# A state-space stage in a two-block kernel: where a branch GEMM and the next group's convolutions stand beside the preludes

## The chip, the cores and the metric

The program runs on one core of one Trainium2 chip as a single launch. The metric is the device time of an execution in microseconds (us). The core's engines each work through a queue of their own in order: TensorE (PE: matmuls and transposes), VectorE (DVE), ScalarE (ACT), GpSimd (POOL) and SyncE (SP, which issues the weight and row transfers). They meet through semaphores. Matmul results lie in PSUM banks, all other tiles in SBUF.

## The reference

512 tokens of width 1024 go through two blocks of two layers each, in float32. The first block (a hybrid mixer with a gated FFN) is not touched. A layer of the second block projects its input, and runs a state-space branch, a differential attention and a memory cross attention, which are gated, summed, projected and normalised. The stage in question is the state-space branch:

```
z, xbc, dt_raw, ... = split(x @ w_in)
xbc = silu(centred_depthwise_conv(xbc, conv_w, conv_b))      # 5 taps
xs, bm, cm = split(xbc)                                      # 32 heads of 64; 4 groups of 128 states
dt = softplus(dt_raw + dt_bias);  a = -exp(a_log)
y  = ssd_scan(xs*dt[fwd], dt[fwd]*a[0], bm, cm)              # chunks of 128 tokens
   + flip(ssd_scan(flip(xs*dt[bwd]), ...))                   # the same, backwards
   + d_skip * xs
y_ssd  = rmsnorm(y * silu(z)) * norm_w
merged = gate0 * (y_ssd @ w_br_ssd) + gate1 * ... + gate2 * ...
```

`ssd_scan` builds, for each chunk, a 128x128 decayed product of `cm` and `bm` that is applied to `xs`, and a state that is carried from chunk to chunk.

## The kernel before

**Layout.** Tiles are feature-major: 128 features on the partitions, the 512 tokens on the free axis. A full-precision GEMM is made of three passes over split operands (high by high L407, high of the weight by low of the input L408, low of the weight by high of the input L409), so a 1024-deep GEMM of one output tile is 24 matmuls of 128x512, and a 512-deep one is 12. Each weight block is loaded by SP into one of three `wraw` buffers, its high part is cast by ACT (L400) and its low part subtracted by DVE (L401).

**The stage.** `ssd` runs the 2048 inner channels in four groups g of 512 (four tiles `f` of 128 each, two heads to a tile). These are its pieces:

- `conv_x(g)`, 4 steps: a GEMM into a `pb` bank (two banks), the middle tap by ACT (L1347) and four taps by DVE (L1352) read from that bank into `svy`, silu by ACT (L1353) into `sxf`. `sxf` has seven buffers.
- `conv_bc(g)`, 2 steps: the same for `sbm` and `scm`, with GEMMs into a `pg` bank (two banks).
- `prelude(g)`, 11 steps. Steps 1 to 4, one for each chunk: four transposes of the `sxf` tiles into a `pb` bank (L429) and a copy by ACT to `sxt` (L1458). Step 5: transposes of `sbm` with a copy to `sbt` (L1465), and `cm`·`bm` products (L1469) which DVE masks (L1471, L1472). Steps 6 to 11, the state chain: DVE scales a chunk of `sxt` (L1481, into `st`, the `st2` buffers, four of them), PE multiplies by `sbt` (L1483, into `pm`), and DVE makes the new state: by a copy for the first one of each direction (L1486), else by adding (L1490) the older state that POOL has decayed (L1489). Directions alternate, three steps each.
- `ftiles(g)`, 16 steps, four for each of four tiles: the z GEMM with a silu (L1507), row loads, per head the decay exponents on ACT (L1517, L1518), min on DVE (L1521), exp on ACT (L1522), the masked product on POOL and DVE (L1519, L1520, L1523); then PE applies it (L1529, 8 matmuls) and the states (L1537, 6 matmuls), DVE, POOL and ACT finish the tile (L1531 to L1554) as a split pair `syp`.
- `branch(g)`, 4 steps of two 512-deep GEMMs each, from the group's four `syp` pairs into `pg` banks, copied by ACT (g = 0, L1565) or added by DVE (L1567) to the eight `merged` tiles `mg`.
- `gate_thread`, 8 gate GEMMs with sigmoid.

**What sets the order.** These pieces are generators. `weave` (L354 to L368) always advances the live one with the smallest `done/total`, and of equals the one that was named first. The order in which instructions are recorded so is their priority for a list scheduler at compile time, which works with costs of its own and may take a later one first where its operands are ready; on the chip each engine then runs its list in order. L1572 to L1592 say what is woven with what: decays with the first group's convolutions; then for each group `prelude(g)` with `branch(g-1)`, `ftiles(g)` with `conv_x(g+1)` (the gates for the last), and `conv_bc(g+1)` alone; then `branch(3)`.

Of the kernel before, what the change touches and what calls it, by code (L numbers as in the profile page):

```python
# [20 lines left out]
KD = 8  # L21
# [1303 lines left out]
def block2(c: Core, io, C, h, out, kvs, stop=None):  # L1325
# [18 lines left out]
    def conv(ps, cw, cb, m, res):  # L1344

        y = c.w(name="svy")
        A.activation(y, ps, AF.Identity, scale=cw[:, 2, m : m + 1], bias=cb[:, m : m + 1])  # L1347
        for tap in (0, 1, 3, 4):
            o = tap - 2
            d = slice(max(0, -o), S - max(0, o))  # L1350
            s = slice(max(0, o), S - max(0, -o))
            V.scalar_tensor_tensor(y[:, d], ps[:, s], cw[:, tap, m : m + 1], y[:, d], op0=ALU.mult, op1=ALU.add)  # L1352
        A.activation(res, y, AF.Silu)  # L1353
# [72 lines left out]
    def ssd(l, h, merged):  # L1426
# [10 lines left out]
        def conv_x(g):  # L1437
            for i in range(4):
                o = c.w(name="sxf")
                conv(proj(l, ("xbc", l, 4 * g + i), h, "pb"), cw, cb, 4 * g + i, o)  # L1440
                grp[g]["xf"].append(o)
                yield

        def conv_bc(g):
            for k, (nm, m) in enumerate((("sbm", 16 + g), ("scm", 20 + g))):
                o = grp[g][nm] = c.w(name=nm)
                conv(proj(l, ("xbc", l, m), h), cw, cb, m, o)
                yield
# [108 lines left out]
        def branch(g):  # L1557
            for j in range(4):
                hi, lo = c.load(("ws", l, g, j), 4)
                for i in range(2):  # L1560
                    m = 2 * j + i
                    ps = c.pg()
                    c.gemm_fm((hi[:, :, i * P : (i + 1) * P], lo[:, :, i * P : (i + 1) * P]), grp[g]["ys"], ps)
                    if g == 0:
                        A.copy(merged[m], ps)  # L1565
                    else:
                        V.tensor_tensor(merged[m], merged[m], ps, op=ALU.add)  # L1567
                yield

        gates = []  # L1570
        th = lambda gen, n: c.thread(gen, n, "S", "pm")
        with c.phase("ssd") as pool:  # L1572
            c.spare, c.spare_turn = pool, cycle(range(3))
            c.weave(th(decays(l, h, cdr, tm, d_fe, d_eo), 6), th(chain(conv_x(0), conv_bc(0)), 6))
            for g in range(4):
                c.weave(th(prelude(g), 11), th(branch(g - 1) if g else iter(()), 4))
                c.weave(th(ftiles(g), 16), th(conv_x(g + 1), 4) if g < 3 else th(gate_thread(l, 0, h, ["sxf"] * KD, gates), 7))
                if g < 3:
                    c.weave(th(conv_bc(g + 1), 2))
            c.weave(th(branch(3), 4))  # L1580
            ps = c.col_sums(sqa)
            v = c.small(NT)
            V.tensor_scalar(v, ps, 1.0 / 2048, 1e-5, op0=ALU.mult, op1=ALU.add)
            rs = c.rsqrt(v, NT)
            rbp = c.pm()
            c.row_bcast(rs, rbp)
            rb = c.w(name="sy1")
            V.tensor_copy(rb, rbp)
            for m in range(KD):
                V.tensor_tensor(merged[m], merged[m], gates[m], op=ALU.mult)  # L1590
                G.tensor_tensor(merged[m], merged[m], rb, op=ALU.mult)
            c.spare = None  # L1592

    def gate_thread(l, br, h, tags, out):
        for m in range(KD):
            out.append(gate(l, br, m, h, tags[m]))
            yield
# [343 lines left out]
    for l in range(DEPTH):  # L1941
# [22 lines left out]
        th = lambda gen: c.thread(gen, 8, "N", "pm")  # L1964
# [5 lines left out]
        else:  # L1970
# [8 lines left out]
            h = hn  # L1979
# [172 lines left out]
```

## Time and profile before

| | |
|---|---|
| three timed runs | 3864.66 to 3871.67 us, median 3867.84 us |
| profiled execution, own time | 3856.39 us |
| its span, first to last instruction | 3854.6 us |
| granted TensorE clock, mean (of 2.4 GHz) | 0.972 |
| PE busy | 3624.0 us, 94% |
| DVE, ACT, POOL busy | 63%, 47%, 20% |
| state-space stage, layer 0 | 1588 to 2046 us |
| state-space stage, layer 1 | 2735 to 3206 us |

A row of the timeline gives the start, the length, engine, line, operation, and in square brackets how long the engine stood idle before it and on what it waited. A row of the view of waits sums such idle time by the waiting line and the one that was waited for. Bank and buffer numbers are left out of the names. In the profile's program, a matmul of f32 operands other than the GEMMs' shows as two records.

### The profile page before, as it was taken

Reading aid. Unit: us, or ns where it says so; the run is one execution under the profiler, and the core shown is the slowest. Engines: PE = TensorE matmul, PEld = TensorE weight load, DVE = VectorE, ACT = ScalarE, POOL = GpSimd, SP = SyncE. Lnnn points to the kernel's source line nnn. Section 1 sums busy time; section 2 is a strip of 40 time slices with the busy share of each in tenths; the row PEclk is TensorE's granted clock in tenths of the full one; section 3 lists DMA queues with packets and bytes.
Section 4 is the critical chain, followed back from the end, with each engine's and each line's share of the span. In section 5 each row is a group of like instructions: output and inputs, shape, how many; then the busy total and the mean of one; then the engine's idle time right before and its main releaser. Section 6 shows DMA issues by size and latency. Waiting matters only on the chain. (4 is left out here: it accounts for less than half of the span.)

```text
span 3854.6 us, 51308 instructions
## 1 busy us (share of the span) xinstructions
PE 3624.0 (94%) x19000; PEld 2984.2 (77%) x19000; DVE 2431.1 (63%) x4355; ACT 1795.0 (47%) x3155; POOL 765.1 (20%) x877
## 2 busy tenths in 40 slices
PE   6888999998899999999999999999999999999998
PEld 4776887787777888777787887877777788887787
DVE  7986645567665333687866674337787766674336
ACT  5432422245323222677654664333776654664332
POOL 2331000003210000143432111003234332111003
PEclk9989999999899999999999999999999999999998
DMA  5711446642113233444433332323443433332222
GB/s 195 187 60 47 145 153 199 201 146 64 50 43 105 97 99 96 124 140 132 130 113 103 92 107 82 103 79 111 143 140 123 131 111 108 94 105 88 93 82 72
DMA packets 167419, 432.91 MB, mean 112 GB/s; under 512 B 30080, under 2 KB 49920, under 8 KB 167168
## 3 DMA queue, kind: packets, MB, share of 16 engines
q1 hardware_dynamic: 167168, 429.62, 36.0%
q8 instruction: 150, 2.46, 0.3%
q14 instruction: 101, 0.83, 0.1%
HBM read 396.24 MB, written 12.32 MB: 106 GB/s over the span
## 5 line engine op out<-in xcount | busy, mean ns | idle before, releaser
L400 ACT CAST whi<-wraw 128x1024 fp32r<-128x1024 f32 (+1 forms) x488 | 506.5, 1039 | 1037.0 <-PE pg L408 842.6
L401 DVE TENSOR_TENSOR wlo<-wraw,whi 128x1024 fp32r<-128x1024 f32 (+1 forms) x488 | 640.9, 1314 | 403.4 <-ACT whi L400 388.6
L407 PE MATMUL pg<-h,whi 128*128 128x512 f32 (+1 forms) x2192 | 876.6, 400 | 15.6 <-ACT h L400 10.7
L409 PE MATMUL pg<-h,wlo 128*128 128x512 f32 (+1 forms) x2192 | 862.0, 393 | 6.6 <-DVE wlo L401 6.6
L408 PE MATMUL pg<-h,whi 128*128 128x512 f32 (+1 forms) x2192 | 862.6, 394 | 4.3 <-POOL h L401 4.3
L407 PEld LDWEIGHTS pg<-h,whi 128*128 128x128 f32 (+1 forms) x2192 | 412.5, 188 | 107.5 <-ACT h L400 13.4
L409 PEld LDWEIGHTS pg<-h,wlo 128*128 128x128 f32 (+1 forms) x2192 | 412.6, 188 | 99.2 <-DVE wlo L401 13.6
L408 PEld LDWEIGHTS pg<-h,whi 128*128 128x128 f32 (+1 forms) x2192 | 412.9, 188 | 94.8 <-POOL h L401 7.4
L407 PE MATMUL pg<-whi,h 128*128 128x256 f32 (+1 forms) x640 | 187.8, 295 | 15.8 <-ACT whi L400 10.9
L408 PE MATMUL pg<-wlo,h 128*128 128x256 f32 (+1 forms) x640 | 186.4, 292 | 11.6 <-DVE wlo L401 11.4
L401 POOL TENSOR_TENSOR gp<-mraw,gp 128x256 fp32r<-128x256 f32 x32 | 25.4, 813 | 864.1 <-ACT gp L400 864.1
L409 PE MATMUL pg<-whi,h 128*128 128x256 f32 (+1 forms) x640 | 184.0, 288 | 0.0
L409 PE MATMUL pg<-gp,wlo 128*128 128x512 f32 (+1 forms) x432 | 159.9, 370 | 0.9 <-DVE wlo L401 0.9
L407 PE MATMUL pg<-gp,whi 128*128 128x512 f32 (+1 forms) x432 | 159.7, 370 | 0.0
L408 PE MATMUL pg<-gp,whi 128*128 128x512 f32 (+1 forms) x432 | 159.6, 369 | 0.0
L407 PE MATMUL pg<-yp,whi 128*128 128x512 f32 (+2 forms) x368 | 142.7, 389 | 6.2 <-ACT whi L400 2.9
L408 PE MATMUL pg<-yp,whi 128*128 128x512 f32 (+2 forms) x368 | 142.8, 389 | 3.6 <-DVE yp L401 3.6
L409 PE MATMUL pg<-yp,wlo 128*128 128x512 f32 (+2 forms) x368 | 142.2, 388 | 2.9 <-DVE wlo L401 2.9
L407 PEld LDWEIGHTS pg<-whi,h 128*128 128x128 f32 x640 | 124.3, 195 | 23.1 <-ACT whi L400 13.1
L1519 POOL TENSOR_SCALAR st<-scl,stm 128x128 f32<-128x128 f32 x256 | 124.2, 504 | 89.5 <-PE pm L1529 89.5
L408 PEld LDWEIGHTS pg<-wlo,h 128*128 128x128 f32 x640 | 124.7, 195 | 16.3 <-DVE wlo L401 14.3
L530 DVE CUSTOM_DVE_ANT_0 wraw<-wraw,cond 128x1024 f32<-128x1024 f32 x80 | 100.7, 1263 | 54.9 <-DMA wraw<-in_wflat_dram 54.8
(585 smaller groups left out, 7601.7 us busy)
## 6 DMA issues: line engine op xcount, KB each, us to landing
wraw<-in_wflat_dram SPq DMA_DIRECT2D x595, 512.0 KB
srf<-dram SPq DMA_DIRECT2D x64, 256.0 KB
sre<-dram SPq DMA_DIRECT2D x64, 256.0 KB
seo<-dram SPq DMA_DIRECT2D x128, 96.0 KB
araw<-in_wflat_dram SPq DMA_DIRECT2D x16, 512.0 KB
rsw<-rr SPq DMA_DIRECT2D x128, 64.0 KB
wraw<-in_wflat_dram SPq DMA_DIRECT2D x16, 384.0 KB
mraw<-in_mem_dram SPq DMA_DIRECT2D x40, 128.0 KB
```

The source lines that it names most:

```text
L400: self.nc.scalar.copy(hi, src)
L401: (eng or self.nc.vector).tensor_tensor(lo, src, hi.bitcast(F32), op=ALU.subtract)
L407: mm(out, ah, bh, start=start, stop=False)
L408: mm(out, ah, bl, start=False, stop=False)
L409: mm(out, al, bh, start=False, stop=stop)
L530: V.tensor_tensor_reduce(r, r, cond, 1.0, 0.0, ALU.mult, ALU.add, mod[:, j : j + 1])
L1519: G.tensor_scalar(t2[:, sl], cbl[:, ch], dtt[:, ch, hh : hh + 1], 1.0, op0=ALU.mult, op1=ALU.mult)
```

## The change

The four pieces that are woven with the tiles are made ahead of the loop (`nxt`). In the first group, `conv_x(1)` is now woven with `prelude(0)`, counted as three steps (`total = 3`), until the prelude ends; what is left of it is woven with the first group's tiles. In the other groups the branch of the group before starts with `done = -1`, so that one of its steps is taken ahead of the prelude's first.

```
         c.weave(th(decays(l, h, cdr, tm, d_fe, d_eo), 6), th(chain(conv_x(0), conv_bc(0)), 6))
+        nxt = [th(conv_x(1), 4), th(conv_x(2), 4), th(conv_x(3), 4), th(gate_thread(l, 0, h, ["sxf"] * KD, gates), 7)]
         for g in range(4):
-            c.weave(th(prelude(g), 11), th(branch(g - 1) if g else iter(()), 4))
-            c.weave(th(ftiles(g), 16), th(conv_x(g + 1), 4) if g < 3 else th(gate_thread(l, 0, h, ["sxf"] * KD, gates), 7))
+            pre = th(prelude(g), 11)
+            if g:
+
+                tb = th(branch(g - 1), 4)
+                tb.done = -1
+                c.weave(pre, tb)
+            else:
+                nxt[0].total = 3
+                c.weave(pre, nxt[0], until=pre)
+                nxt[0].total, nxt[0].done = 4 - nxt[0].done, 0
+            c.weave(th(ftiles(g), 16), nxt[g])
             if g < 3:
                 c.weave(th(conv_bc(g + 1), 2))
```

With prelude steps P1 to P11, branch steps B1 to B4 and convolution steps X1 to X4, the recorded order changes as follows. First group: before P1 to P11, later one X with each tile; now P1 X1 P2 to P4 X2 P5 to P8 X3 P9 to P11, and X4 with the first tile. Other groups: before P1 B1 P2 P3 B2 P4 to P6 B3 P7 to P9 B4 P10 P11; now B1 P1 B2 P2 P3 B3 P4 to P6 B4 P7 to P11.

What the scheduler made of it stands below at three places; "..." is for rows left out. On PE, the first group's prelude in layer 0 (`sxf`, `sbm`: operands of transposes; `h` with `pg_13889` or `pg_14006`: the first tile's z GEMM). Before, the transposes and the start of the z GEMM:

```order
L429 MATMUL pb_13795<-k_1_60,sxf_13509 128x128
...
L429 MATMUL pb_13795<-k_1_60,sxf_13666 128x128
L429 MATMUL pb_13802<-k_1_60,sxf_13509 128x128
...
L429 MATMUL pb_13809<-k_1_60,sxf_13509 128x128
...
L429 MATMUL pb_13809<-k_1_60,sxf_13666 128x128
L407 MATMUL pg_13889<-h_13320,whi_13892 128x512
L429 MATMUL pb_13816<-k_1_60,sxf_13509 128x128
...
L408 MATMUL pg_13889<-h_13320,whi_13892 128x512
...
L429 MATMUL pb_13824<-k_1_60,sbm_13711 128x128 x4
```

Now, with two GEMMs of the second group's convolutions (`pb_13803`, `pb_13863`) among the same transposes:

```order
L429 MATMUL pb_13795<-k_1_60,sxf_13509 128x128
...
L429 MATMUL pb_13795<-k_1_60,sxf_13666 128x128
L407 MATMUL pb_13803<-h_13320,whi_13806 128x512
...
L409 MATMUL pb_13803<-h_13341,wlo_13807 128x512
L429 MATMUL pb_13841<-k_1_60,sxf_13509 128x128
...
L429 MATMUL pb_13841<-k_1_60,sxf_13666 128x128
L407 MATMUL pg_14006<-h_13320,whi_14009 128x512
...
L408 MATMUL pg_14006<-h_13329,whi_14009 128x512
L429 MATMUL pb_13848<-k_1_60,sxf_13509 128x128
...
L409 MATMUL pg_14006<-h_13329,wlo_14010 128x512
...
L407 MATMUL pb_13863<-h_13320,xhi_13866 128x512
...
L429 MATMUL pb_13902<-k_1_60,sbm_13711 128x128 x4
```

The first and second convolution GEMM stand within the transposes, and the third and fourth follow among and behind the state matmuls, all ahead of the first tile's L1529; before, the first of them stood right ahead of that L1529, and each of the others with one of the next tiles. By the whole list, ACT's table loads in the program go from 211 to 221, six of the added ones in the last group of layer 0; every other engine has the same instructions as before.

On PE, the start of the fourth group in layer 0 (`sxf`: transposes; `syp`: the third group's branch GEMMs). Before:

```order
L409 MATMUL pg_16421<-h_13341,xlo_16425 128x512
L429 MATMUL pb_16459<-k_1_60,sxf_15812 128x128
...
L429 MATMUL pb_16500<-k_1_60,sxf_15812 128x128
...
L429 MATMUL pb_16507<-k_1_60,sxf_15812 128x128
...
L429 MATMUL pb_16548<-k_1_60,sxf_15812 128x128
...
L429 MATMUL pb_16548<-k_1_60,sxf_16286 128x128
L407 MATMUL pg_16472<-syp_15901,whi_16468 128x512
L408 MATMUL pg_16472<-syp_15901,whi_16468 128x512
```

Now:

```order
L409 MATMUL pg_16421<-h_13341,xlo_16425 128x512
L429 MATMUL pb_16493<-k_1_60,sxf_15812 128x128
...
L429 MATMUL pb_16493<-k_1_60,sxf_16286 128x128
L429 MATMUL pb_16534<-k_1_60,sxf_15812 128x128
L429 MATMUL pb_16534<-k_1_60,sxf_15970 128x128
L407 MATMUL pg_16465<-syp_15901,whi_16461 128x512
...
L409 MATMUL pg_16465<-syp_16375,wlo_16462 128x512
L429 MATMUL pb_16534<-k_1_60,sxf_16128 128x128
...
L429 MATMUL pb_16541<-k_1_60,sxf_15812 128x128
...
L429 MATMUL pb_16541<-k_1_60,sxf_16128 128x128
L407 MATMUL pg_16479<-syp_15901,whi_16461 128x512
```

The branch GEMMs, which followed all sixteen transposes, now stand after six of them and after eleven. Layer 1's fourth group has the same two orders, and its third group went from eleven ahead of the first GEMM to seven. Layer 0's third group had six ahead of its first GEMM, and four between that and the second, before; it has seven and three now.

On PE, the end of the state chain in the third group of layer 0 (`st` with `sbt`: the state matmuls; `syp`: branch; `h`: the first tile's z GEMM). Before:

```order
L409 MATMUL pg_15663<-syp_15441,wlo_15646 128x512
L1483 MATMUL pm_15679<-st_3347_15677,sbt_15621 128x512
L1483 MATMUL pm_15685<-st_3350_15683,sbt_15621 128x512
L1483 MATMUL pm_15693<-st_3354_15691,sbt_15621 128x512
L407 MATMUL pg_15705<-syp_14967,whi_15701 128x512
...
L409 MATMUL pg_15719<-syp_15441,wlo_15702 128x512
L1483 MATMUL pm_15735<-st_3363_15733,sbt_15621 128x512
L1483 MATMUL pm_15743<-st_3367_15741,sbt_15621 128x512
L407 MATMUL pg_15755<-h_13320,xhi_15758 128x512
```

Now:

```order
L409 MATMUL pg_15697<-syp_15441,wlo_15680 128x512
L1483 MATMUL pm_15713<-st_3352_15711,sbt_15655 128x512
L1483 MATMUL pm_15719<-st_3355_15717,sbt_15655 128x512
L1483 MATMUL pm_15727<-st_3359_15725,sbt_15655 128x512
L1483 MATMUL pm_15735<-st_3363_15733,sbt_15655 128x512
L407 MATMUL pg_15755<-h_13320,xhi_15758 128x512
...
L409 MATMUL pg_15755<-h_13326,xlo_15759 128x512
L1483 MATMUL pm_15743<-st_3367_15741,sbt_15655 128x512
L407 MATMUL pg_15755<-h_13329,xhi_15758 128x512
```

The 24 branch matmuls (22 of their rows are left out above) that stood between the third state matmul and the last two are gone from there, and nine of the z GEMM's stand ahead of the last one. On DVE, at the same place (`shs`: states; `st_3367`: the last state matmul's operand). Before:

```order
L401 TENSOR_TENSOR wlo_15817<-wraw_15814,whi_15816 128x1024
L1486 COPY shs_15681<-pm_15679 128x512
L1490 TENSOR_TENSOR shs_15687<-shd_15688,pm_15685 128x512
L1490 TENSOR_TENSOR shs_15695<-shd_15696,pm_15693 128x512
L1481 TENSOR_TENSOR st_3367_15741<-sxt_15571,stm_13471 128x512
L1520 SCALAR_TENSOR_TENSOR st_3380_15792<-scu_15634,stm_13470,st_3380_15792 128x128 x4
```

Now:

```order
L401 TENSOR_TENSOR wlo_15917<-wraw_15914,whi_15916 128x1024
L1486 COPY shs_15715<-pm_15713 128x512
L1490 TENSOR_TENSOR shs_15721<-shd_15722,pm_15719 128x512
L1490 TENSOR_TENSOR shs_15729<-shd_15730,pm_15727 128x512
L1490 TENSOR_TENSOR shs_15737<-shd_15738,pm_15735 128x512
L1481 TENSOR_TENSOR st_3367_15741<-sxt_15605,stm_13471 128x512
L1520 SCALAR_TENSOR_TENSOR st_3380_15792<-scu_15668,stm_13470,st_3380_15792 128x128 x4
```

One more state addition stands ahead of the last scaling (L1481). The second to fourth groups of both layers have this new pattern, six places in all.

## Rows read from the trace of the kernel before

**Rows 1.** The page's first part: busy time of PE and its weight loads.
```profile
PE 3624.0 (94%) x19000; PEld 2984.2 (77%) x19000; DVE 2431.1 (63%) x4355; ACT 1795.0 (47%) x3155; POOL 765.1 (20%) x877
```
**Rows 2.** Windows: length, then busy of PE, PEld, DVE, ACT, POOL; clock; DMA.
```profile
1621.00:1705.00 84.00, 78.46 (x405) 62.00 (x404) 74.27 (x116) 68.41 (x131) 39.19 (x51) 0.98 0.45 134
2766.00:2852.00 86.00, 78.29 (x401) 61.01 (x399) 77.05 (x117) 70.12 (x136) 38.81 (x51) 0.98 0.43 133
1656.00:1705.00 49.00, 44.55 (x239) 36.61 (x238) 43.69 (x64) 45.32 (x89) 19.25 (x20) 0.97 0.59 172
```
**Rows 3.** Waits of PE, first group of layer 0, 1621 to 1705 us.
```profile
PE pm L1529 <- DVE st L1523: 2.7, 1, 2.7
PE pg L407 <- DVE svy L1352: 1.6, 1, 1.6
```
**Rows 4.** Waits of PE, first group of layer 1, 2766 to 2852 us.
```profile
PE pm L1529 <- DVE st L1523: 2.7, 3, 2.1
PE pg L407 <- DVE svy L1352: 2.3, 2, 1.9
```
**Rows 5.** Waits of PE, later groups of layer 0: total, times, longest.
```profile
PE pg L407 <- DVE svy L1352: 5.7, 1, 5.7
PE pb L429 <- ACT sxt L1458: 3.5, 1, 3.5
PE pb L429 <- ACT sxf L1353: 3.3, 1, 3.3
```
**Rows 6.** Waits of PE, later groups of layer 1, 2853 to 3206 us.
```profile
PE pb L429 <- ACT sxt L1458: 8.8, 2, 5.3
PE pb L429 <- ACT sxf L1353: 6.4, 2, 4.8
```
**Rows 7.** Timeline of PE, starts of the third and fourth group, layer 0.
```profile
1805.30 0.77 PE L407 MATMUL pg<-syp,whi 128*128 128x512 f32 x1 [5.66 <-DVE svy L1352]
...
1906.77 1.33 PE L429 MATMUL pb<-k,sxf 128*128 128x128 f32 x5 [3.34 <-ACT sxf L1353]
1911.60 1.97 PE L429 MATMUL pb<-k,sxf 128*128 128x128 f32 x8 [3.50 <-ACT sxt L1458]
1913.72 0.80 PE L407 MATMUL pg<-syp,whi 128*128 128x512 f32 x1
```
**Rows 8.** Timeline of DVE, start of the fourth group, layer 0.
```profile
1908.55 1.53 DVE L1352 SCALAR_TENSOR_TENSOR svy<-pg,c,svy 128x510 f32<-128x510 f32 x2 [0.44 <-ACT svy L1347]
...
1912.92 1.40 DVE L1352 SCALAR_TENSOR_TENSOR svy<-pg,c,svy 128x510 f32<-128x510 f32 x2
```
**Rows 9.** Groups of instructions by line: DVE, state-space stage of layer 0.
```profile
L401 DVE TENSOR_TENSOR wlo<-wraw,whi 128x1024 fp32r<-128x1024 f32 x42 | 56.6, 1350 | 14.7 <-ACT whi L400 14.7
L1352 DVE SCALAR_TENSOR_TENSOR svy<-pb,c,svy 128x511 f32<-128x511 f32 (+1 forms) x63 | 46.7, 742 | 9.4 <-ACT svy L1347 9.2
```
**Rows 10.** Timeline of PE, state chain of the third group, layer 0.
```profile
1828.36 2.73 PE L1483 MATMUL pm<-st,sbt 128*128 128x512 f32 x6
1830.53 0.79 PE L407 MATMUL pg<-syp,whi 128*128 128x512 f32 x1
...
1836.40 1.88 PE L1483 MATMUL pm<-st,sbt 128*128 128x512 f32 x4
```
**Rows 11.** Timeline of DVE, the same state chain.
```profile
1832.41 0.69 DVE L1490 TENSOR_TENSOR shs<-shd,pm 128x512 f32<-128x512 f32 x1 [0.58 <-POOL shd L1489]
1833.02 0.93 DVE L1481 TENSOR_TENSOR st<-sxt,stm 128x512 f32<-128x512 f32 x1
```
**Rows 12.** Timeline of POOL, the same state chain.
```profile
1831.32 2.08 POOL L1489 TENSOR_TENSOR shd<-shs,scd 128x512 f32<-128x512 f32 x2 [5.11 <-DVE shs L1486]
```
**Rows 13.** Timeline of ACT, a table load and what follows it.
```profile
1894.87 1.28 ACT L1522 ACT_TABLE_LOAD   x1
1896.16 0.63 ACT L1522 ACTIVATE sre<-sre 128x512 f32<-128x512 f32 x1
```
**Rows 14.** Windows, as rows 2: last group's tiles of layer 0.
```profile
1945.00:1998.00 53.00, 53.00 (x285) 43.79 (x284) 40.51 (x61) 38.15 (x65) 20.38 (x31) 1.00 0.46 144
```

## Prediction

> **What bounds the kernel now.** I read the busy shares first: PE is busy 3624.0 us of a span of 3854.6 [rows 1], so it sets the time, and reordering pays only where PE stands idle. I then took the view of waits for PE, stretch by stretch through the state-space stage. Three kinds of wait are there to be won or lost.
>
> In the first group, PE waits for the products of a tile (L1529 for L1523) 2.7 us in each layer, and for a `pg` bank that the taps of `conv_bc` still read 1.6 and 2.3 us [rows 3, 4]. The windows of this group say what stands behind: 84 us with PE busy 78.46 and DVE 74.27, and 86 us with 78.29 and 77.05 [rows 2]. DVE is as good as full in layer 1, and in the tiles (1656 to 1705 us, 49 us) PE has 44.55, DVE 43.69 and ACT 45.32: all three are near their limit.
>
> At the starts of the later groups PE waits for the last convolution's silu (`sxf`), for the copy that frees a `pb` bank (`sxt`), or for the taps that free a `pg` bank: 5.7 + 3.5 + 3.3 = 12.5 us in layer 0 and 8.8 + 6.4 = 15.2 us in layer 1 [rows 5, 6]. These are the largest waits that the change touches.
>
> The third kind is absent: at the end of the state chain the last two state matmuls start right behind the 24 branch matmuls, without idle time [rows 10].
>
> **The change part by part.** No engine but ACT gets another instruction, so each term is a wait that goes, stays or comes.
>
> *First group.* Three of four convolution GEMMs leave the stretch behind L1529 of the first tile; the first stood ahead of it already. A GEMM of 24 matmuls takes 5.87 us, read from the 24 between 1830.53 and 1836.40 [rows 10], so 17.6 us of PE's work leave the tiles. With them go 4 x 0.742 + 1.35 = 4.3 us of DVE's work each [rows 9], 13.0 us in three. Does the prelude have holes for it? Hardly: the waits listed for this group lie in the tiles and at its end, and the z GEMM and the first convolution were in the prelude already. So work is exchanged: the prelude grows by what the tiles lose. In the tiles the `conv_bc` GEMMs, recorded behind them, are drawn forward as cover for PE, so that their taps are done earlier; the wait for their `pg` bank at the group's end should go. That is 1.6 in layer 0 and 1.9 (the longest of the two) in layer 1: **-3.5 us**. The waits of L1529 I leave as they are: the tile's row work still ends last. Bounds: all waits of rows 3 and 4 go, 4.3 + 5.0 = -9.3; or the tiles fall to the pace of DVE, 17.6 - 13.0 = 4.6 in each layer, +9.2. SP's loads for the three GEMMs go out earlier too, ahead of the tiles' row loads; three `wraw` buffers hold them, and I cost this at nothing as long as the tiles' rows, which are asked for as before, come in time. One buffer matters: `sxf` has seven, so the silu of the fourth convolution waits for the first tile's L1531, with ACT's queue behind it. That is part of the upper bound.
>
> *Starts of the later groups.* The branch GEMMs move to between the transposes. A branch GEMM needs a `pg` bank, and both banks hold `conv_bc` results that DVE is still tapping: at the fourth group of layer 0 DVE is at these taps from 1908.55, and a pair of them still runs at 1912.92 to 1914.32 [rows 8]. PE's first branch GEMM starts at 1913.72 [rows 7]. So when it is asked for after six transposes, at about 1908, it can hardly start sooner than it did behind sixteen; the wait of 3.50 for the copy becomes a wait for taps, and the ten transposes left come behind it. By that replay the start costs 1 or 2 us more. Another row says the contrary: the third group of layer 0 has had the new order all along, and pays 5.66 for the taps [rows 7] and next to nothing besides, against 3.34 + 3.50 = 6.84 at the fourth group. If the three starts in the old order (6.84 in layer 0, 15.2 for two in layer 1) came down to 5.7 to 6 each, that would be -4.0. I take half: **-2 us**. Bounds: all of 22.0 goes, for banks that are free in time; or +2 at each of three, +6.
>
> *State chain.* Here a cover is taken away. Call S the start of the first state matmul of the last batch, 1828.36. Before, three state matmuls end the batch at S + 2.17 and 24 branch matmuls follow until S + 8.04 [rows 10]. In that time DVE makes two additions and the last scaling, which ends at 1833.95, S + 5.6 [rows 11]: 2.4 us to spare. Now PE has four state matmuls, 4 x 0.72 = 2.9 us, and nine of the z GEMM's, 9/24 of 5.87 = 2.2 us, and wants the last one at S + 5.1. And DVE has one addition more ahead of the scaling; it needs the second decay by POOL, which ended at 1831.32 + 2.08 = 1833.40 [rows 12]. So the addition runs from 1833.40 to 1834.1 (0.69), the scaling to 1835.0 (0.93): S + 6.6. PE waits 6.6 - 5.1 = 1.5 us, and what is queued behind it is the rest of the z GEMM and, through it, the first tile. There are six such places: 9 us if all are alike. The trace shows one chain, with DVE held up by a weight split just ahead of it; where no split stands there, DVE is ahead and nothing is lost. Bounds 0 and +9; I take the middle, **+4.5 us**.
>
> *ACT's table loads.* Ten more are in the list, six of them in the last group of layer 0. In the trace the load takes 1.28 us and the exp behind it starts at 1896.16, one hundredth after its end [rows 13]. In that group's tiles ACT has 38.15 us of 53.00 [rows 14]; with 6 x 1.28 = 7.7 it has 45.9, still under PE's 53. Nothing. The Trainium skill (*ScalarE: Activation LUTs*, section *What ACT_TABLE_LOAD costs*) adds a drain to each switch and comes to about 2.66 us; by that estimate the six would bring ACT to 54.1 us, 1.1 us over PE's, and the sum would be 1.1 us longer. The trace has no such gap between load and exp, so the row is followed.
>
> *Sum.* -3.5 - 2 + 4.5 = -1.0 us. The durations are those of the profiled execution, whose own time of 3856.39 us (span 3854.6, 1.8 us around it) is 11.45 us under the median of the timed runs, 3867.84. A change in waits carries over as it is: 3867.84 - 1.0 = 3866.8, about **3867 us**.
>
> **The rivals.** *The starts are covered (faster).* If a branch GEMM between the transposes gives ACT time for the copies, the waits for `sxt` go, 3.5 + 8.8 = 12.3 us. For it: at 1911.60 PE waits 3.50 us for a copy while branch matmuls lie ready. Against it: the bank that DVE frees no sooner. With -3.5 in the first group and the chain at half its middle value, +2.3: -12.3 - 3.5 + 2.3 = -13.5, 3854 us.
>
> *The first group's tiles lose their cover (slower).* The mechanism is DVE's and ACT's pace in the tiles once the convolution GEMMs are gone from there: they keep 4.6 us more than PE in each layer, PE idles in front of L1529, and DVE at 77.05 of 86 us has no room to have worked ahead in the prelude. Price 9.2, with the chain at 4.5 and nothing won at the starts: +13.7, 3882 us. It decides where the waits in front of the first group's L1529 pass some 6 us a layer, against 2.7 now. For it: the tight windows. Against it: in the prelude the heads' rows can be made ahead, as far as their buffers go.
>
> *Nothing moves.* The scheduler had drawn the z GEMM and the first convolution into the prelude already, and the third group of layer 0 had nearly the new order; the rest may just exchange one wait for another of the same length. 3868 us.
>
> **How the numbers follow.** Below 0.2%, 7.7 us, this kernel's measurement tells no change. I give my forecast 0.38, with a range of its own of 3860 to 3875; the faster rival 0.31, the slower one 0.22, nothing moving 0.09. Faster by over 0.2%: nearly all of the faster rival (0.29) and 0.04 of the forecast, 0.33. Slower: 0.20 of the slower rival and 0.03 of the forecast, 0.23. The rest, 0.44, is no change that can be told. The outer bounds are -9.3 - 22 = -31.3 and 9.2 + 6 + 9 = +24.2; for 8 in 10 the range reaches to the rivals and a little past the faster one, 3850 to 3883 us.
>
> **What would show it.** In the changed kernel's waits of PE: for the first group, no wait for taps at its end, and L1529's near 2.7 us a layer (above 6, the slower rival). For the fourth group of layer 0, a branch GEMM that starts near 1913.7 less the shift up to there, with a wait for L1352 in front of it (if it starts two us or more sooner, the faster rival). At each of the six chains, a wait of L1483 for L1481 of about 0.8 us on the mean; none at all would strike that term, 1.5 at each would double it. A prediction off by more than a few us in either direction, with the waits of PE in this stage unchanged, would mean that something else than these three places decides, such as transfers that come later for SP's changed order.

## The result, and the profile after

The changed kernel takes 3908.55 us, median of four runs (3906.87 to 3913.39), against 3866.25 us, median of four, for the kernel before: a ratio of 1.0116, with a 95% interval of 1.0101 to 1.0130. That is 42 us slower, outside the predicted range of 3850 to 3883 us.

The page's first part, after, beside [rows 1]: of the span's 57 us more (3911.6, against 3854.6), PE is busy 30 us longer for the same 19000 records, and idle 27 us longer.

```profile
PE 3654.2 (93%) x19000; PEld 3005.2 (77%) x19000; DVE 2430.0 (62%) x4355; ACT 1809.8 (46%) x3165; POOL 763.2 (20%) x877
```

To see where, I cut the stage at places that have the same work ahead of them in both lists. The table is worked out from the timelines of PE; each pair is layer 0 / layer 1, in us. "First group" runs from its first transpose to the second group's first L1529; the next two from one group's first L1529 to the next one's; "last group" from its first L1529 to the first L451 behind the branch.

| kernel | first group | second | third | last group | sum |
|---|---|---|---|---|---|
| before | 123.8 / 127.1 | 104.1 / 104.8 | 105.9 / 107.5 | 87.9 / 87.9 | 421.7 / 427.3 |
| after | 132.2 / 147.4 | 104.6 / 104.5 | 105.4 / 107.3 | 94.2 / 92.9 | 436.3 / 452.1 |
| branch_first | 125.1 / 127.6 | 106.4 / 105.4 | 105.8 / 106.5 | 92.7 / 94.5 | 429.9 / 434.0 |
| branch_first_g12 | 125.1 / 127.6 | 105.8 / 105.4 | 105.3 / 105.2 | 88.0 / 87.9 | 424.1 / 426.1 |
| branch_first_gate_exp | 125.1 / 128.8 | 106.2 / 106.1 | 106.1 / 106.0 | 92.5 / 91.4 | 430.0 / 432.3 |
| branch_first_dve_mult | 123.4 / 125.9 | 103.8 / 103.7 | 104.1 / 103.9 | 90.7 / 90.9 | 421.9 / 424.3 |
| conv_early | 130.9 / 144.4 | 105.1 / 104.5 | 107.0 / 107.0 | 87.9 / 88.0 | 430.9 / 443.9 |
| one_conv_early | 132.3 / 134.5 | 104.4 / 103.9 | 106.6 / 106.9 | 87.9 / 88.0 | 431.3 / 433.2 |
| conv_early_dve_mult | 127.6 / 134.9 | 102.4 / 103.5 | 103.1 / 103.7 | 87.5 / 87.5 | 420.7 / 429.7 |
| conv_early_z_exp | 133.6 / 138.9 | 109.4 / 107.8 | 106.8 / 106.1 | 88.6 / 89.0 | 438.4 / 441.8 |
| after_dve_mult | 128.9 / 135.6 | 104.3 / 101.9 | 104.2 / 105.4 | 90.7 / 90.7 | 428.1 / 433.5 |
| after_dve_chain | 130.1 / 137.7 | 100.3 / 101.9 | 101.0 / 101.5 | 87.5 / 87.5 | 419.0 / 428.5 |
| before_dve_mult | 122.0 / 127.9 | 104.0 / 102.9 | 104.1 / 103.1 | 87.5 / 87.5 | 417.6 / 421.5 |
| before_dve_chain | 118.8 / 127.2 | 100.8 / 102.0 | 100.5 / 100.7 | 87.5 / 87.5 | 407.7 / 417.4 |
| branch_in_pm | 123.1 / 126.1 | 96.9 / 96.6 | 102.9 / 103.0 | 91.9 / 91.9 | 414.9 / 417.6 |

The stage is 14.6 + 24.8 = 39.4 us longer, nearly all of the 42 us by which the medians differ. The first group loses 8.4 and 20.2 us, the last group 6.3 and 5.0. (A group's row holds the start and the state chain of the group behind it.) The second and third groups, with the starts and state chains that two of the three terms of the prediction were about, are even within 0.6 us. (The two profiled executions differ by another 18 us ahead of and behind the stage, where the instructions are the same; the medians do not show that.)

**The first group.** The windows of its prelude and its tiles, layer 0 and then 1, and the last group's tiles of layer 0 (columns as in [rows 2]):

```profile
1627.00:1665.00 38.00, 36.45 (x161) 27.46 (x160) 29.37 (x44) 23.78 (x41) 12.17 (x20) 1.00 0.21 69
1665.00:1716.00 51.00, 41.64 (x237) 31.95 (x237) 42.89 (x68) 35.51 (x70) 24.65 (x31) 1.00 0.49 144
2786.00:2830.00 44.00, 37.38 (x160) 28.43 (x159) 31.78 (x45) 28.06 (x52) 12.16 (x20) 0.96 0.27 82
2830.00:2884.00 54.00, 46.51 (x235) 36.34 (x234) 42.47 (x69) 33.76 (x66) 23.58 (x30) 0.87 0.41 132
1969.00:2034.00 65.00, 60.88 (x324) 49.44 (x323) 36.20 (x48) 47.12 (x70) 23.30 (x28) 0.97 0.39 121
```

In layer 0 the prelude takes 38 us where it took 21, by its three GEMMs of about 5.5 us each, 16.6 us. The tiles (first L1529 to the end of their GEMMs) take 50 where they took 59.5, so only 9.5 of the 16.6 us come back. DVE is busy 42.9 of 51 us and ACT 35.5, so neither is full, and PE idles 9 us. PE's waits in these tiles of layer 0, to be read against [rows 3]:

```profile
PE pm L1529 <- DVE st L1523: 3.2, 3, 1.4
PE pg L409 <- DVE xlo L401: 3.1, 1, 3.1
PE pg L409 <- DVE wlo L401: 1.6, 1, 1.6
PE pg L407 <- ACT szs L1507: 1.5, 1, 1.5
```

And in the first group of layer 1, beside [rows 4]:

```profile
PE pb L429 <- ACT sxt L1458: 9.2, 2, 5.8
PE pm L1529 <- DVE st L1523: 5.2, 3, 2.9
```

The whole first group, before and after in layer 0 and then in layer 1 (columns as in [rows 2]), shows that the two layers lose in different ways:

```profile
1621.30:1745.00 123.70, 118.16 (x577) 92.68 (x575) 101.66 (x160) 93.20 (x172) 52.17 (x71) 0.99 0.42 126
1627.20:1759.30 132.10, 119.62 (x577) 90.86 (x575) 104.01 (x159) 91.12 (x169) 51.68 (x71) 1.00 0.38 114
2765.80:2892.90 127.10, 119.19 (x577) 92.39 (x575) 106.66 (x165) 95.49 (x182) 51.78 (x71) 0.99 0.42 127
2786.00:2933.40 147.40, 128.75 (x579) 98.75 (x577) 105.44 (x162) 95.45 (x181) 50.10 (x71) 0.92 0.34 107
```

The columns hold PE's busy time; the rest of the length is its idle time. In layer 0 the idle time rises by 6.9 us and the busy time by 1.5. In layer 1, 10.7 us are idle time, and 9.6 us are slower matmuls, at a granted clock of 0.92 in place of 0.99. And of layer 1's idle time much lies outside the tiles: in its prelude PE waits 5.83 us for the copy that frees a `pb` bank.

```profile
2799.29 1.97 PE L429 MATMUL pb<-k,sxf 128*128 128x128 f32 x8 [5.83 <-ACT sxt L1458]
```

```profile
2798.67 0.57 ACT L1458 COPY sxt<-pb 128x512 f32<-128x512 f32 x1
```

ACT does not stand still there (busy 5.64 us of the 5.70 ahead of 2799.2): row work, an exp with a table load, the middle tap of the convolution that now stands in the prelude, and a silu with a table load come ahead of the copy in its list. Every kernel below that has the three convolutions early has this wait (5.8 to 6.0 us); the kernel before waits 1.3 us for that copy.

In the tiles, it is not one wait but four that add up, and they lie on one round: the chain from one tile's L1529 through DVE, POOL and ACT to the next tile's. It can be read in layer 0, engine by engine. PE applies the products of the second tile at 1680.94 and those of the third at 1696.88, 15.9 us later, with 1.40 us of idle time just before (another wait of this round stands in front of a weight split):

```profile
1680.94 1.09 PE L1529 MATMUL pm<-st,sxt 128*64 128x128 f32 x14
...
1696.88 1.09 PE L1529 MATMUL pm<-st,sxt 128*64 128x128 f32 x14 [1.40 <-DVE st L1523]
```

DVE, between the two: L1531 takes the result at 1682.06, and the second L1540 waits 2.62 us for POOL:

```profile
1682.06 0.75 DVE L1531 SCALAR_TENSOR_TENSOR sy<-sxf,c,pm 128x512 f32<-128x512 f32 x1
...
1686.19 0.56 DVE L1540 TENSOR_TENSOR so<-pm,seo 128x384 f32<-128x384 f32 x1 [2.62 <-POOL sy L1541]
...
1696.15 0.68 DVE L1523 TENSOR_TENSOR st<-sre,st 128x512 f32<-128x512 f32 x1
```

POOL: the eight row products of the tile after, released by the same L1529, go first, 3.26 us; only behind them come the two additions, the first of which DVE waits for, and then the multiplication by silu(z):

```profile
1681.92 3.26 POOL L1519 TENSOR_SCALAR st<-scl,stm 128x128 f32<-128x128 f32 x8 [5.89 <-PE pm L1529]
1685.16 1.00 POOL L1541 TENSOR_TENSOR sy<-sy,so 128x384 f32<-128x384 f32 x1
1686.83 1.04 POOL L1541 TENSOR_TENSOR sy<-sy,so 128x384 f32<-128x384 f32 x1 [0.67 <-DVE so L1540]
1687.95 1.80 POOL L1544 TENSOR_TENSOR szs<-sy,szs 128x512 f32<-128x512 f32 x1
```

ACT: the scaling L1546 has waited 2.82 us for that multiplication, and behind it in ACT's list stand a square, the next z's silu with a table load, and the exp with another:

```profile
1689.78 0.72 ACT L1546 ACTIVATE syp<-szs,c 128x512 fp32r<-128x512 f32 x1 [2.82 <-POOL szs L1544]
1690.41 0.61 ACT L1553 ACTIVATE ssq<-szs 128x512 f32<-128x512 f32 x1
1691.04 1.28 ACT L1507 ACT_TABLE_LOAD   x1
1692.33 0.60 ACT L1507 ACTIVATE szs<-pg 128x512 f32<-128x512 f32 x1
1692.94 1.28 ACT L1522 ACT_TABLE_LOAD   x1
1694.24 0.63 ACT L1522 ACTIVATE sre<-sre 128x512 f32<-128x512 f32 x1
```

The exp at 1694.24 is what DVE's L1523 at 1696.15 multiplies with (DVE has other work up to then), and that releases the next L1529. A round takes some 15 us, of which POOL has 7. Before, the tiles followed each other at 1642.29, 1658.93, 1673.99 and 1687.93, about as far apart; but there PE had a z GEMM, a convolution GEMM and 2.4 us of small matmuls in each, 13.5 us, and stood still for 2.74 us once [rows 3]. So by these rows the round was as long before, and what went is the PE work that covered it.

**The last group.** PE now waits for the gates' sigmoid, which keeps a `pg` bank (4.1 of the 6.3 us in layer 0):

```profile
PE pg L407 <- ACT sxf L1363: 4.1, 2, 2.5
```

ACT's list shows why the sigmoid at 1983.69 is late, and with it the GEMM on PE:

```profile
1978.72 0.72 ACT L1546 ACTIVATE syp<-szs,c 128x512 fp32r<-128x512 f32 x1 [2.60 <-POOL szs L1544]
1979.36 0.62 ACT L1553 ACTIVATE ssq<-szs 128x512 f32<-128x512 f32 x1
...
1981.34 1.03 ACT L400 CAST whi<-wraw 128x1024 fp32r<-128x1024 f32 x1
1982.39 1.28 ACT L1363 ACT_TABLE_LOAD   x1
1983.69 0.69 ACT L1363 ACTIVATE sxf<-pg,c 128x512 f32<-128x512 f32 x1
```

```profile
1984.43 0.50 PE L407 MATMUL pg<-h,xhi 128*128 128x512 f32 x1 [1.64 <-ACT sxf L1363]
```

ACT stands 2.60 us in front of the scaling, which waits for POOL, and only then comes to the row work, the weight cast and the gate. In the list of before, a gate and most of the row work stood ahead of that scaling, and it waited 0.81 us:

```profile
1960.56 0.69 ACT L1363 ACTIVATE sxf<-pg,c 128x512 f32<-128x512 f32 x1
...
1964.11 0.72 ACT L1546 ACTIVATE syp<-szs,c 128x512 fp32r<-128x512 f32 x1 [0.81 <-POOL szs L1544]
```

**Starts and state chains.** PE's last state matmul of the second group, and the first branch GEMM of the third and fourth, layer 0:

```profile
1749.37 1.13 PE L1483 MATMUL pm<-st,sbt 128*128 128x512 f32 x2 [1.00 <-DVE st L1481]
...
1819.29 0.77 PE L407 MATMUL pg<-syp,whi 128*128 128x512 f32 x1 [5.24 <-DVE svy L1352]
...
1925.04 0.77 PE L407 MATMUL pg<-syp,whi 128*128 128x512 f32 x1 [6.27 <-DVE svy L1352]
```

The chain's wait is 1.00 us in all six places. The starts of the third and fourth group wait 5.24 and 6.27 us for the taps, where [rows 7] had 5.66 and 6.84. In layer 1 they wait 12.6 us in all, where [rows 6] had 15.2.

### The profile page after: what moved, and what is told of

Its sections match the earlier page's. It is cut to its first block, busy times and chain, and to the rows that moved or that the text cites. A ratio compares the mean times of both kernels' runs of the same rounds, so it can differ in the third digit from the quotient of the medians.

```text
span 3911.6 us, 51298 instructions
## 1 busy us (share of the span) xinstructions
PE 3654.2 (93%) x19000; PEld 3005.2 (77%) x19000; DVE 2430.0 (62%) x4355; ACT 1809.8 (46%) x3165; POOL 763.2 (20%) x877
## 5 line engine op out<-in xcount | busy, mean ns | idle before, releaser
L409 PE MATMUL pg<-h,wlo 128*128 128x512 f32 (+1 forms) x2192 | 864.9, 395 | 11.3 <-DVE wlo L401 11.2
L407 PEld LDWEIGHTS pg<-whi,h 128*128 128x128 f32 x640 | 126.7, 199 | 21.8 <-ACT whi L400 11.8
L530 DVE CUSTOM_DVE_ANT_0 wraw<-wraw,cond 128x1024 f32<-128x1024 f32 x80 | 100.3, 1258 | 62.2 <-DMA wraw<-in_wflat_dram 62.2
L408 PEld LDWEIGHTS pg<-wlo,h 128*128 128x128 f32 x640 | 127.1, 199 | 14.5 <-DVE wlo L401 12.6
```

What stands on the lines that cost most here:

```text
L407: mm(out, ah, bh, start=start, stop=False)
L408: mm(out, ah, bl, start=False, stop=False)
L409: mm(out, al, bh, start=False, stop=stop)
L530: V.tensor_tensor_reduce(r, r, cond, 1.0, 0.0, ALU.mult, ALU.add, mod[:, j : j + 1])
```

## The experiments

Theory A, formed on these traces, says that the tiles' round through POOL and ACT sets the pace where PE has too little to cover it: in the first group through the convolutions' early start, in the last through the new order of ACT's list. Its rivals are B, by which the branch at the second group's start makes the first group's loss, and C, by which DVE's whole work paces the tiles. For the last group A1 blames the additional table loads, and A2 the wait in front of the scaling. Ratios are to the kernel before on the same chip, with 95% intervals.

**1. branch_first.** The second half of the change alone.

```
                 else:
-                    nxt[0].total = 3
-                    c.weave(pre, nxt[0], until=pre)
-                    nxt[0].total, nxt[0].done = 4 - nxt[0].done, 0
+                    c.weave(pre)
```

> Only the second half of the change: one branch step ahead of the prelude in the second to fourth groups; the first group as before. Theory A (the tiles of the first group keep a pace of their own, 14 to 16 us each, so that GEMMs moved out of them are lost time; and the gates of the last group are held up on ACT by table loads that the branch-first order brings): only the last group's loss is left, +11 us (6.3 in layer 0 and 5.0 in layer 1 by the traces), with waits of PE for the gates' sigmoid as in the changed kernel. Rival B (the loss in the first group is made at its end, where the branch now stands ahead of the transposes): +25 to +40 us, nearly the whole loss.

Measured: 3874.34 us, ratio 1.0047 (1.0030 to 1.0065). The table has 4.8 and 6.6 us of loss in the last group and 1.3 and 0.5 in the first. Theory A expected this, and B is out.

**2. conv_early.** The first half alone.

```
-                tb.done = -1
```

> Only the first half: the second group's convolutions woven with the first group's prelude; branch and preludes as before. Theory A: the first group's loss alone, +28 us (8.4 in layer 0, 20.2 in layer 1), with waits of PE in front of L1529 and of the z GEMMs in the tiles, and none for the gates. Rival B: less than +10 us.

Measured: 3883.73 us, ratio 1.0065 (1.0050 to 1.0080), with a loss of 7.1 and 17.3 us in the first group; the last group is as before. So the first group's loss comes from the early convolutions. The two halves add up to the whole: 0.47% and 0.65% against 1.16%.

**3. branch_first_g12.** The second half, without the fourth group.

```
-                tb.done = -1
+                tb.done = -1 if g < 3 else 0
```

(on top of branch_first)

> The second half alone, and only in the second and third groups; the fourth group's prelude starts as before. ACT's list for the last group has the table loads of before again (14 in place of 18 up to the end of the gates). Theory A: no loss, 0 with 4 us to either side, since the starts and the state chains came out even. If it is the branch at the start of the second group that costs (rival B): still +20 us or more.

Measured: 3867.97 us, ratio 1.0011 (0.9997 to 1.0024), no change that can be told. The last group is at 88.0 and 87.9 us again. So it is the branch step ahead of the fourth group's prelude that brings the last group's loss.

**4. one_conv_early.** A smaller dose.

```
-                    nxt[0].total = 3
+                    nxt[0].total = 1
```

(on top of conv_early)

> The first half alone with a smaller dose: one convolution recorded in the prelude (the scheduler then puts two of the four ahead of the first tile, one more than before, where the change puts four). Theory A: each GEMM taken from the tiles costs about a third of the first group's loss, +9 us; between +4 and +13. Rival C (no loss until DVE's or ACT's whole work in the tiles is longer than PE's): 0, within 3 us.

Measured: 3874.74 us, ratio 1.0043 (1.0027 to 1.0058). The first group loses 8.5 and 7.4 us with one GEMM taken, and the whole is outside both expectations, so the loss does not go by the number of GEMMs. In layer 0 one GEMM costs as much as three; but there PE's busy time has risen by 4.6 us (122.8 us at a granted clock of 0.96, where conv_early has 119.6 at 1.00), and its idle time by 4.0 against conv_early's 5.8.

**5. branch_first_gate_exp.** The gates' sigmoid replaced by exp.

```
-        A.activation(g, ps, AF.Sigmoid, bias=...)
+        A.activation(g, ps, AF.Exp, bias=...)
```

(on top of branch_first)

> The second half of the change alone (as in branch_first), and the gates' sigmoid replaced by exp, so that the gates need no table of their own beside the row work's exp; the gates' values are other ones by that. Theory A1 (the last group's loss is made by the additional table loads that stand on ACT between the gates and the row work): the stretch from the last group's first L1529 to the sum of squares, 67.4 us before and 72.2 and 74.0 in branch_first, comes back to 67.4 with 0.6 to either side, and PE waits for no gate; in time -11 us against branch_first. Rival A2 (ACT stands in front of the tile's scaling, which waits for POOL, and the gates are queued behind that): the stretch stays above 70 and the waits for the gates stay.

Measured: ratio 1.0030 (1.0016 to 1.0044); the last group still takes 92.5 and 91.4 us. The gates' own loads are gone, and PE waits as follows in the last group of layer 0:

```profile
PE pg L407 <- ACT sxf L1363: 2.2, 2, 1.9
PE pg L407 <- ACT szs L1507: 1.5, 1, 1.5
```

What ACT waits for there, in this kernel and then in branch_first:

```profile
ACT syp L1546 <- POOL szs L1544: 18.0, 4, 6.9
```

```profile
ACT syp L1546 <- POOL szs L1544: 14.0, 4, 4.6
```

The time that the loads had is now spent waiting for POOL at the scaling, 18.0 us where it was 14.0. So A1 is out as the main cause in layer 0; taking the loads away is worth 0.2 us there and 3.1 in layer 1.

**6. conv_early_dve_mult.** The multiplication by silu(z) moved from POOL to DVE.

```
-                G.tensor_tensor(yz, y1, zs, op=ALU.mult)
+                V.tensor_tensor(yz, y1, zs, op=ALU.mult)
```

(on top of conv_early)

> The first half of the change alone (as in conv_early), and the multiplication of a tile by silu(z) done by DVE (0.7 us) where POOL takes 1.76 us for it. Theory A (the first group's tiles follow each other at the length of a round through PE, DVE, POOL, ACT and back to DVE): the round gets about 1 us shorter, the first group's tiles 3 to 5 us shorter in each layer, 6 to 10 us faster than conv_early. Rival C (DVE's whole work paces the tiles, 42.9 us busy of 51): 4 times 0.7 us more of it, 2 to 3 us longer in each layer.

Measured: 3859.38 us, ratio 0.9999 (0.9986 to 1.0013), 24 us less than conv_early, more than either side expected. The first group is 3.3 and 9.5 us shorter although DVE has more to do, which is against C; of the 9.5, 3.9 are PE's busy time, at a granted clock of 0.95 where it was 0.92. The second and third groups gain too, 1 to 4 us each.

**7. conv_early_z_exp.** The silu of z replaced by exp.

```
-                A.activation(zs, proj(l, ("z", l, f), h), AF.Silu)
+                A.activation(zs, proj(l, ("z", l, f), h), AF.Exp)
```

(on top of conv_early)

> The first half of the change alone (as in conv_early), and the silu of z replaced by exp, so that no table load stands between z and the row work of a tile; y has other values by that. Theory A: two loads of 1.28 us leave the round of each tile but the first, the first group's tiles get 5 to 8 us shorter in each layer. Rival C (DVE's work paces them, which does not change here): within 1.5 us of conv_early in this stretch.

Measured: ratio 1.0096 (1.0079 to 1.0113), slower than conv_early. The first group is 2.7 us longer in layer 0 and 5.5 shorter in layer 1, and the later groups are longer. With another table the scheduler put ACT's list in another order, so this says little on the loads and decides nothing.

**8. after_dve_mult and branch_first_dve_mult; before_dve_mult.** The edit of 6 on top of the changed kernel, of branch_first, and of the kernel before.

> The whole change, and the multiplication of a tile by silu(z) on DVE in place of POOL. In the last group ACT's list is as in the changed kernel, its table loads too (18), with ACT's scaling of a tile ahead of a cast and a gate. Theory A2 (what holds the gates is the round of a tile: ACT stands in front of the scaling until POOL has multiplied, and the gates and weight casts queue behind it; the loads only add to it): the wait gets some 1 to 1.5 us shorter per tile, the last group's stretch falls from 94.2 and 92.9 us to 88 to 90, and the first group's tiles shorten as in conv_early_dve_mult; in all 25 to 40 us faster than the changed kernel, 3870 to 3885 by its own median. Rival A1 (the loads alone): the last group's stretch stays within 1 us; 20 us or less.

Measured: 3884.09 us, ratio 1.0056 (1.0042 to 1.0070). ACT has the same number of table loads from the last group's first L1529 on (15 and 14, where the kernel before has 10 and 9), and the last group falls to 90.7 us in both layers. That is for A2, though its 88 to 90 us are not reached. The first group falls by 3.3 and 11.8 us.

> The second half of the change alone, with the same move from POOL to DVE. A2: the last group's stretch falls from 92.7 and 94.5 us to 88 to 90, the starts of the groups get 1 to 3 us shorter each as the last tile's split pair is done earlier; 3848 to 3858 us, at or under the kernel before. A1: last group as in branch_first, 3862 us or more.

Measured: 3861.45 us, ratio 0.9998 (0.9983 to 1.0012); last group 90.7 and 90.9 us. The time is 3 us above what A2 said, since the last group of each layer stays 3 us over the kernel before with the same edit.

> The kernel before with that move alone, to see what of conv_early_dve_mult's gain is the move's own. If PE covers the tiles' round in the kernel before, the tiles do not change, and only the starts of the groups gain, 1 to 3 us each, six of them: -6 to -15 us. Then conv_early still costs 6 to 15 us beside it. If the round paces the tiles there too, more: -20 us.

Measured: 3857.52 us, ratio 0.9984 (0.9973 to 0.9995), -6 us by the ratio. Beside this control the changed kernel with the same edit costs 27 us, where it costs 42 without.

**9. after_dve_chain, before_dve_chain.** The two additions on DVE as well.

```
-                    G.tensor_tensor(y1[:, sl], y1[:, sl], o1, op=ALU.add)
+                    V.tensor_tensor(y1[:, sl], y1[:, sl], o1, op=ALU.add)
```

(on top of the edit of 6)

> The whole change, with the two additions and the multiplication of each tile all on DVE, so that POOL has nothing in the round from one tile's L1529 to the next one's but the row products. Theory A (the round paces the first group's tiles; POOL's additions stand behind 3.3 us of row products): the stretch of the first group's tiles, 50.1 and 53.6 us in the changed kernel and 46.2 and 47.8 with the multiplication moved, falls by 2 to 4 us more in each layer, and the last group's waits for gates by 1 to 2. 3868 to 3880 us. Rival C (DVE's pace): DVE gets 8 more operations of 0.55 us in each group, and the stretch grows by 2 to 4 us in each layer.

Measured: 3865.23 us, ratio 1.0012 (0.9997 to 1.0027). The last group is at 87.5 us in both layers, its loss gone, with the same 15 and 14 table loads, and PE waits for no gate: that the round through POOL held the gates is shown. The first group is not shorter than in after_dve_mult (130.1 and 137.7 against 128.9 and 135.6). In layer 0 its tiles look shorter, 40.6 us against 46.2, but 20 matmul records fewer stand in them (218 against 238): PE is busy 35.6 us there against 41.2, and idle 5.0 and 5.1. So the additions on DVE gave these tiles nothing. DVE is busy 36.5 of the 40.6 us, 90%, so for this kernel rival C is not excluded. What ACT waits for in these tiles, in transfers:

```profile
ACT srf L1518 <- DMA srf<-dram: 6.2, 2, 4.6
ACT sre L1517 <- DMA sre<-dram: 1.4, 1, 1.4
```

And SP's queue, which issues them, itself waits for buffers that DVE frees:

```profile
SPq L1513 <- DVE st L1523: 8.0, 4, 3.4
SPq L1505 <- DVE st L1520: 5.6, 2, 4.6
SPq L1512 <- DVE sre L1521: 5.0, 2, 4.2
```

So with POOL out of the round, the row buffers and their transfers may be next; no run takes them away by themselves.

> The kernel before with the same moves, as the control. PE covers the round here (its tiles hardly wait), so only the starts of the groups can gain, by the earlier split pair of the last tile: within 6 us of before_dve_mult, either way. If theory A holds, the change's cost beside this control is smaller than the 42 us it costs beside the kernel before and than the 27 us beside before_dve_mult.

Measured: 3838.38 us, ratio 0.9948 (0.9929 to 0.9966), by the ratios 14 us under before_dve_mult (19 by the medians, which are of two chips), which I had not expected. The stage is 14 us shorter, 0.9 to 3.6 us in each of the four middle stretches and 3.2 in layer 0's first group. In the middle stretches the tiles stand 13.47 us apart as in the kernel before, so the gain is at the starts; in layer 0's first group the tiles are 3.3 us shorter, so there PE had not covered the round as I thought. Beside it the changed kernel with the same edits still costs 27 us, and PE's idle time in the first group is still 17 us longer, where it was 18 without the edits. So POOL's part does not explain the first group's loss.

**10. branch_in_pm, branch_in_pm_dve_mult, branch_in_pm_dve_chain.** On top of branch_first_g12, and with the edits of 6 and 9.

```
-                    ps = c.pg()
+                    ps = c.pm() if j < 2 else c.pg()
```

> A version meant to gain: first group as before; one branch step ahead of the prelude in the second and third groups only, so that the last group keeps the table loads of before; and the first four of the eight branch GEMMs write to the four pm banks, which are free between tiles and prelude, and not to the pg banks, which hold the conv_bc results. The theory of the starts (a branch GEMM can't start before DVE has finished the taps on a pg bank, wherever it stands in the list): the waits for L1352, 5.2 to 6.3 us at each start of a third and fourth group, go or come down to the wait for the last tile's split pair, 3 to 4 us less at each of the starts, -12 to -20 us against before. Rival (the wait only changes its name, to the copies and silus of ACT or the split pair of the last tile): within 4 us of before.

Measured: 3838.35 us, ratio 0.9945 (0.9925 to 0.9964), -22 us. PE's waits from the second group to the fourth's start in layer 0, where [rows 5] has 12.5 us for the three kinds, and where branch_first_g12, which differs in the bank alone, waits 12.4 us for the taps:

```profile
PE pb L429 <- ACT sxt L1458: 4.1, 1, 4.1
PE pm L1483 <- DVE st L1481: 1.1, 1, 1.1
PE pb L429 <- ACT sxf L1353: 0.2, 1, 0.2
```

The waits for the taps (L1352) are gone; the second group's stretch, up to the third's first L1529, is 7.2 and 8.2 us shorter, and the fourth group's start keeps 4.1 us for a copy. (The last group's stretch has 4 us more, without idle time: work of the start that now follows in it.) So the starts were held by the `pg` bank.

> The faster version branch_in_pm with the move. In it the starts wait no longer for a pg bank but for copies and the last tile's split pair, so an earlier multiplication should give its 1 us per start, and the third and fourth group's are the ones left with waits (4.4 and 5.0 us): -4 to -10 us against branch_in_pm. If the starts wait for ACT's copies alone: no change within 2 us.

Measured: 3833.94 us, ratio 0.9937 (0.9922 to 0.9952), 4 us under branch_in_pm by the medians, which is within the intervals of both.

> The faster version, branch_in_pm, with the same moves. Its tiles are covered by PE, and its starts wait 1 us at the second and third group and 3 to 4 at the fourth: -2 to -6 us against branch_in_pm_dve_mult if the last tile's split pair is what the fourth group's start waits for; within 2 us, or slower, if ACT's or DVE's queues are.

Measured: 3831.08 us, ratio 0.9927 (0.9911 to 0.9942), the fastest of all: 22 to 34 us under the kernel before (0.58% to 0.89% of 3858 us). Against branch_in_pm_dve_mult the 3 us are within the intervals of both.

## Why the prediction was wrong, point by point

- **First group, -3.5 us: this step failed.** It took the exchange of 17.6 us of PE's work between prelude and tiles as free, and costed the bound at DVE's work (4.6 us a layer). Measured: +8.4 and +20.2 us, of which 1.0 each is the second group's state chain; conv_early alone has +7.1 and +17.3. The wait for taps that was to be won did go in both layers; it was the exchange that cost. A view of busy shares can't show it, since in the changed kernel DVE is busy 84% of the tiles' time and no engine is full; the tiles follow each other by a round through four engines, and that could have been read from the trace of before, where the tiles are 14 to 16.6 us apart and PE's own work fills 13.5 of that. Two more costs of the exchange stood in no term: in layer 1 the copy that frees the prelude's `pb` bank came 5.83 us late behind ACT's added work, and the matmuls behind such waits ran at a lower granted clock (9.6 us). Moving POOL's multiplication out of the round takes 3.3 and 11.8 us back (8), where the same edit gives the first group of the kernel before 1.8 us and nothing. Beside a control with the same edits, 15 us (with the multiplication moved) and 22 us (with the additions too) of the first group's 28.6 us stay. So it is shown that the early convolutions make the loss and where PE waits, but what paces the tiles stays open: row buffers and transfers are late in the trace of 9, DVE is at 90% there, and neither was taken away by itself.
- The slower rival named the place, the direction and the sign to look for (waits in front of L1529 of over 6 us a layer; they are 3.2 and 5.2, the rest stands in front of weight splits, silu and copies), but its price, 9.2 us, was a third of the 28.6 measured, and it blamed the pace of DVE and ACT. 6 speaks against DVE's.
- **ACT's table loads in the last group, nothing: this step failed too.** The loads added to the last group are four in each layer, not six in layer 0 alone, and taking the gates' loads away gives 0.2 us in layer 0 and 3.1 in layer 1 (5). But with them ACT's list had changed its order, with the scaling ahead of casts and gates, and its wait for POOL came in front of PE's GEMMs: +11.3 us. I compared ACT's busy time with the stretch and did not follow the list. The Trainium skill's drain (*ScalarE: Activation LUTs*, *What ACT_TABLE_LOAD costs*) is not seen here either: at 1691.04 the load takes 1.28 us and the silu starts at 1692.33.
- **Starts, -2 us: right in kind, a little small.** A branch GEMM asked for earlier waited for the same taps, 5.24 and 6.27 us where 5.66 and 6.84 were lost before. With layer 1 the four starts gain 3.6 us, near the 4.0 of which the prediction took half. 10 shows that the bank was the reason.
- **State chain, +4.5 us: right in mechanism and size.** 1.00 us at each of six places, 6.0 in all.
- "Nothing moves" held for the sum of the second and third group, where the starts' gain and the chains' loss are about equal.

## What to carry to other kernels

When GEMMs are moved out of a loop of small dependent steps, compare the loop's round, followed engine by engine from one release to the next, with the PE work that is left in it; here PE, DVE and ACT were busy 82, 84 and 70% of such tiles, and none was full. Look as well at what the GEMMs' own small steps on other engines now stand in front of, in the place that they are moved to. Where a scheduler writes the queues, look at what each engine's list now has behind an instruction that waits, not only at the instructions that were added. The wait for a bank was not won by asking earlier; another bank won it, and gave this kernel 22 us.

## What the runs showed of the hardware

After PE had stood still for 5.83 us in layer 1's prelude, its granted clock was 0.50 from 2799.30 to 2801.00 us, the lower of its two levels (1.2 of 2.4 GHz), and 1.00 again from 2803; the eight transposes there take 1.97 us, where eight took 1.03 in layer 0 before. In layer 1's tiles, which follow, PE stood still four more times, for 0.59 to 2.85 us, and the granted clock is 0.87 on the mean; from 2867 to 2874, behind waits of 2.33 and 0.59 us, it is 0.51. Over the whole program PE's busy time rose by 30 us for the same instructions.
